# The second half's S5 scan steps, queued behind the last step of the first half's

## The chip, the core and the metric

The kernel runs on one core of one Trainium2 chip, in one launch. The metric is device time in microseconds, the median of several runs. A second number is the profiled execution: one run recorded by the hardware profiler, which gives start, length and releaser of nearly every instruction. The engines named here are TensorE (PE, matrix products into PSUM), VectorE (DVE), ScalarE (ACT), GpSimd (POOL) and SyncE (SP, which issues most loads and stores). Each engine runs its instructions in the order in which they were queued and stops at the first one that has to wait.

## What is computed

One layer of a hybrid backbone over 1024 latent tokens of width 1024, with 256 context tokens ahead of them. Its mixer has two groups, an RG-LRU group and an S5 group; an output projection, a layer norm, a squared-ReLU MLP and a second layer norm follow. The change is in the S5 group. Each of its 64 channel groups of 16 drives a complex diagonal state of 64, forward and backward:

```python
def s5_direction(u_ctx, u_lat, ...):
    lam_bar = jnp.exp(lam * dt)
    def run(u, h0):
        bu = einsum('blgh,gph->blgp', u, b_bar)
        h, h_fin = linear_scan(a, bu, h0, reverse)   # h[t] = a * h[t-1] + bu[t]
        return einsum('blgp,ghp->blgh', h, c_mat).real, h_fin
    y_ctx, h_fin = run(u_ctx, 0)
    y_lat, _ = run(u_lat, h_fin)

s5 = gelu(yl_f + yl_b + d_skip * s_lat)
s5_lat = s5 * sigmoid(s5 @ s5_glu_w + s5_glu_b)      # the GLU
out = concat([rg_lat, s5_lat]) @ w_out + b_out
```

## The kernel before

Products that need more precision than one pass are split: a weight or input x is stored as a high part `h` (a cast by ScalarE, as `wh`) and a low part `l = x - h` (by VectorE, as `wl`), and TensorE adds three products of the parts.

The S5 sequence is cut into chunks of 8 tokens, 32 chunks of context and 128 of latent tokens. TensorE first makes each chunk's contribution to the state (`s5_in`), which lies in two tiles, H0 for the first 32 channel groups and H1 for the other 32. `scan(hf)` then runs over the chunks of one half on VectorE. The 32 context chunks are combined as a tree (tiles `sC`). The latent chunks come one after the other, 127 steps for each half, and each step is three small instructions that need each other's results: `sT` = a * h[i-1], `sU` = the sum of two parts of `sT`, and h[i] = `sU` + h[i].

`s5_states(m)` copies the states of block m out of H0 (m = 0 to 3) or H1 (m = 4 to 7) into a tile `h2`: four copies for each block, all on ScalarE for H0, and half on ScalarE and half on VectorE for H1. `s5_out(m)` multiplies them on TensorE (`ps_so`), applies gelu on ScalarE (`gs`), transposes on TensorE (`ps_gt`), and splits the result into high (ScalarE) and low (VectorE) parts in G0 or G1. G0 takes the memory of H0 and G1 that of H1. The first two output blocks of the GLU are accumulated as the blocks of G come (`ps_gl`); these stand in TensorE's queue between the S5 outputs.

While the scans run, TensorE has other work: the gate projections (`proj_gate`, whose results `ge` VectorE multiplies and SyncE stores), and then the RG-LRU half of the output projection. Its inputs `mh0` to `mh7` are split like weights. Its output blocks are made as the first two together (`k_outer`), four one by one (`prod`), and blocks 6 and 7 together again. Each result in PSUM (`ps_wo`, two buffers for each tag) is evicted by ScalarE to a tile `pt` (`put_part`).

The order on each engine is not the order of the code. A scheduler places every instruction by its own estimate of the times; program order decides between instructions only in part. `with after(x)` tells it that what is issued inside must be queued behind the instruction x. It does not reorder anything while the kernel runs.

Of the kernel before, what the change touches and what calls it, by code (L numbers as in the profile page):

```python
# [15 lines left out]
P = 128  # L16
# [10 lines left out]
GH = 32  # L27
# [14 lines left out]
def build(nc, tc, a, out):  # L42
    V, S, G, PE = nc.vector, nc.scalar, nc.gpsimd, nc.tensor
    MUL, ADD, SUB, MAX = ALU.mult, ALU.add, ALU.subtract, ALU.max

    def tt(o, x, y, op, eng=None):
        (eng or V).tensor_tensor(out=o, in0=x, in1=y, op=op)  # L47
# [13 lines left out]
    def after(ins):  # L61
        return nullcontext() if ins is None else tc.issue_after(ins.ins)
# [120 lines left out]
    def tmp(w=64, dt=F32):  # L183
        cnt[0] += 1
        return pp.tile([P, row(w)], dt, name=f"t{cnt[0]}")[:, 0:w]

    def exp_(v, w):
        k, r, h, e = tmp(w), tmp(w), tmp(w), tmp(w)
        ts(k, v, 1.0 / math.log(2.0), MUL, -127.0, MAX)
        ts(k, k, 127.0, ALU.min, 12582912.0, ADD)  # L190
        ts(k, k, 12582912.0, SUB)
        stt(r, k, -0.693145751953125, v, MUL, ADD)
        stt(r, k, -1.42860682030941723212e-6, r, MUL, ADD)
        ts(r, r, 0.5, ALU.min, -0.5, MAX)
        ts(h, r, 1.0 / 40320, MUL)
        for n in (5040, 720, 120, 24, 6, 2, 1):
            stt(h, h, 1.0 / n, r, ADD, MUL)
        ts(h, h, 1.0, ADD)
        ts(k, k, 127.0, ADD, 8388608.0, MUL)
        ei = tmp(w, I32)  # L200
        V.tensor_copy(ei, k)
        tt(e, h, f(ei), MUL)
        return e
# [77 lines left out]
    u, z, z2, acc = tmp(16), tmp(16), tmp(16), tmp(16)  # L281
    S.activation(u, lam, AF.Abs)
    ts(u, u, -1.0, MUL)
    u = exp_(u, 16)
# [22 lines left out]
    for k in range(KT):  # L307
# [18 lines left out]
        for r, src, pl_, n in ((0, xr, xlp, NL), (1, xc, xcp, NC)):  # L326
            h = pl_.tile([P, n], F32R, name=f"x{r}h{k}")
            lo = pl_.tile([P, n], F32R, name=f"x{r}l{k}")
            t = sup.tile([P, n], F32, tag=f"xt{r}", name="xt", bufs=1)
# [262 lines left out]
    def s5_in(m):  # L592
        ub = inp.tile([P, 8, NCH], F32, tag="ub", name="ub", bufs=2)
        ld(ub, uscr[m].rearrange("t (c g) n -> (t c) g n", g=8))
        for q in range(2):
            xt = inp.tile([P, 4, 2, P], F32, tag="xt", name="xt", bufs=3)
            in_ld[m] = ld(xt, xscr[m, q])
            for g in range(4):
# [6 lines left out]
                cp(hv[64:128, :, 0:CC], ps[64:128, :, CC - 1::-1])  # L605
                cp(hv[64:128, :, CC:NCH], ps[64:128, :, NCH - 1:CC - 1:-1])

    def scan(hf):
        h = H[hf]
        hs = slice(hf * GH, (hf + 1) * GH)  # L610

        for q in range(5):
            d = 1 << q
            for o in range(0, CC, 16 * d):
                n = min(8, (CC - o) // (2 * d))
                lo, hi = (h[:, o + e:o + e + 2 * d * (n - 1) + 1:2 * d] for e in (d - 1, 2 * d - 1))
                t = [pst.tile([P, 8, 2, GH], F32, tag="tr", name="sC", bufs=2)[:, 0:n] for _ in range(2)]
                tt(t[0], a8[:, q, 0:1, hs].unsqueeze(1).to_broadcast([P, n, 2, GH]), lo, MUL)
                tt(t[1], a8[:, q, 1:3, hs].unsqueeze(1).to_broadcast([P, n, 2, GH]), lo, MUL)
                tt(hi, t[0], hi, ADD)  # L620
                tt(hi, t[1][:, :, ::-1, :], hi, ADD)
        al = sc.tile([P, 2, 2, GH], F32, tag=f"al{hf}", name=f"al{hf}", bufs=1)
        V.tensor_copy(al[:, 0], a8[:, 0, 0:1, hs].to_broadcast([P, 2, GH]))
        V.tensor_copy(al[:, 1], a8[:, 0, 1:3, hs])
        for i in range(CC, NCH - 1):
            t = sc.tile([P, 2, 2, GH], F32, tag=f"sT{hf}", name="sT", bufs=2)
            tt(t, al, h[:, i - 1:i].to_broadcast([P, 2, 2, GH]), MUL)
            u = sc.tile([P, 2, GH], F32, tag=f"sU{hf}", name="sU", bufs=2)
            tt(u, t[:, 0], t[:, 1, ::-1, :], ADD)
            tt(h[:, i], u, h[:, i], ADD)  # L630


    def proj_gate(m):
# [95 lines left out]
    def s5_states(m):  # L729
        h2 = h2s[m] = sop[m % 4 // 3].tile([P, 8, 2, CL], F32, tag="h2", name="h2", bufs=3 if m % 4 < 3 else 1)  # L730
        for q in range(2):
            starts(H[m // 4], h2[:, 4 * q:4 * q + 4], (m % 4) * 8 + 4 * q, V.tensor_copy if m >= 4 else S.copy)

    def s5_out(m):
        if m % 2 == 0:
            mtt[m // 2] = sop[1].tile([P, 16, P], F32, tag="mt", name="mt", bufs=2)
            kv = kpscr[m // 2].rearrange("m (g c) x -> c (m g) x", g=8)
            for t in range(T8):
                ld(mtt[m // 2][16 * t:16 * t + 16], kv[:, :, (8 - t) * 16:(8 - t) * 16 + P])
        mt = mtt[m // 2][:, 8 * (m % 2):8 * (m % 2) + 8]  # L740
        u2 = sop[1].tile([P, 8, CL], F32, tag="u2", name="u2", bufs=3)
        ld(u2, uscr[m].rearrange("t (c g) n -> (t c) g n", g=8)[:, :, CC:NCH])
        yf = sop[1].tile([P, 2, 2, 4, P], F32, tag="yf", name="yf", bufs=3)
        ld(yf, yscr[m])
        h2 = h2s[m]
        gs = sc.tile([P, T8, 8, 16], F32, tag="gs", name="gs", bufs=2)
        for s in range(2):
            ps = psx.tile([P, 4, P], F32, tag="si", name="ps_so", bufs=2)
            for g in range(4):
                gl = 4 * s + g  # L750
                PE.matmul(ps[:, g, :], u2[:, gl, :], mt[:, gl, :], start=True, stop=False)
                PE.matmul(ps[:, g, :], h2[:, gl, 0, :], yf[:, s, 0, g, :], start=False, stop=False)
                PE.matmul(ps[:, g, :], h2[:, gl, 1, :], yf[:, s, 1, g, :], start=False, stop=True)
            S.activation(gs[:, :, 4 * s:4 * s + 4].rearrange("n t g c -> n g t c"),
                         ps.rearrange("n g (t c) -> n g t c", t=T8), AF.Gelu_apprx_tanh)
        hl = glin[m]
        for j in range(2):
            pt = pst.tile([P, 4, P], F32, tag="tr", name="ps_gt", bufs=2)
            for t in range(4):
                PE.transpose(pt[:, t, :], gs[:, 4 * j + t].rearrange("n g c -> n (g c)"), ident)  # L760
            pf = pt.rearrange("p t n -> p (t n)")
            S.copy(hl[:, 0, HS[j]], pf)
            tt(hl[:, 1, HS[j]], pf, f(hl[:, 0, HS[j]]), SUB)

    for hf in range(2):
        if hf == 0:
            scan(0)
        for m in range(4 * hf, 4 * hf + 4):
            s5_states(m)
        if hf == 0:  # L770
            scan(1)

        g = hp_[hf].tile([P, 5, 2, NL], F32R, tag="h", name=f"G{hf}", bufs=1)
        for m in range(4):
            glin[4 * hf + m] = g[:, m]
        for m in range(4):
            s5_out(4 * hf + m)
# [294 lines left out]
    for p in range(0, NP1 + 4, 2):  # L1072
# [7 lines left out]
        for e in range(2):  # L1080
# [3 lines left out]
            t = ap_.tile([P, 512], F32, tag="r", name="p2", bufs=3)  # L1084
# [75 lines left out]
    def rt():  # L1160
        return ap_.tile([P, 512], F32, tag="r", name="r", bufs=3)
# [5 lines left out]
    for n, p in stream:  # L1167
# [4 lines left out]
        if n == "1":  # L1172

            h = a2.tile([P, 4, 512], F32, tag="hq", name="hq", bufs=2)
            u = a1.tile([P, 2, 512], F32, tag="u", name="u", bufs=2)
            v, t = p2t.pop(p), rt()
# [272 lines left out]
def program(arrays):  # L1449
    import concourse.bacc as bacc  # L1450

    nc = bacc.Bacc("TRN2", target_bir_lowering=False, num_devices=1, dynamic_dma_scratch_size=1024)
    aps = {n: nc.dram_tensor(f"in_{n}", v.shape, mybir.dt.from_np(v.dtype), kind="ExternalInput").ap() for n, v in arrays.items()}
    out = nc.dram_tensor("out_0", (D, NL), F32, kind="ExternalOutput").ap()
    with tile.TileContext(nc) as tc:
        build(nc, tc, aps, out)
    return nc
# [10 lines left out]
```

## Time and profile before

| | us |
|---|---|
| median of 3 runs | 1590.09 (1587.28 to 1592.53) |
| profiled execution | 1590.72 |
| its span, first to last instruction | 1588.9 |
| TensorE busy | 1481.7 (93%) |
| VectorE busy | 1241.8 (78%) |
| ScalarE busy | 859.1 (54%) |

The time outside the span is 1.8 us. A busy share is an average over stages, so it says which engine to follow and not where time is lost. For that one reads the stretches and the waits of single instructions. In a row of the timeline the number in brackets at the end is the idle time of the engine ahead of that instruction and what ended it. Rows that begin before the row above has ended are normal, since the instructions of an engine are pipelined; the distance from start to start is the time that an instruction takes from the queue.

### The profile page before, as it was taken

To read this page: it belongs to the slowest core of one execution; us is meant where nothing else is said; L and a number is where in the kernel's file an instruction comes from. 1 tells how busy PE (TensorE), PEld (TensorE's weight loads), DVE (VectorE), ACT (ScalarE), POOL (GpSimd) and SP (SyncE) were. 2 spreads that over 40 slices of the span, in tenths; PEclk is the share of its full clock that TensorE was granted. 3 is DMA by queue.
4 is the path that set the end of the run, shared out by engine and by line. 5 is a ranking of instruction groups with operands and counts; after the bars stand their busy time and mean duration, and the time that the engine had idled before them with its cause. 6 is when DMAs were issued, how large, how long until landed. Compare 5 with 4: busy or idle time off the path is not lost. (4 is left out here: it accounts for less than half of the span.)

```text
span 1588.9 us, 20498 instructions
## 1 busy us (share of the span) xinstructions
PE 1481.7 (93%) x7148; PEld 1207.3 (76%) x7148; DVE 1241.8 (78%) x2523; ACT 859.1 (54%) x1210; POOL 54.1 (3%) x101
## 2 busy tenths in 40 slices
PE   7899998999978999699999898999999999999997
PEld 2687777778866878598878666877887788888787
DVE  7899899999876989644978788777876556757867
ACT  4676656676795331964233467555656544344325
POOL 0000000000000000000000011010111000000000
PEclk9999999999999999899999899999999999999998
DMA  7623333323664762983768576999997876776603
GB/s 257 230 95 118 104 112 110 106 104 133 218 222 141 199 192 96 251 186 122 241 209 276 153 237 218 311 294 295 290 303 199 312 266 214 260 253 198 230 7 106
DMA packets 143831, 312.56 MB, mean 197 GB/s; under 512 B 16496, under 2 KB 47728, under 8 KB 142320
## 3 DMA queue, kind: packets, MB, share of 16 engines
q1 hardware_dynamic: 104048, 237.45, 46.4%
q10 hardware_dynamic: 31360, 52.83, 8.9%
q0 software_dynamic: 8320, 20.98, 6.0%
q8 instruction: 56, 0.92, 0.2%
q14 instruction: 47, 0.39, 0.1%
HBM read 227.91 MB, written 83.30 MB: 196 GB/s over the span
## 5 line engine op out<-in xcount | busy, mean ns | idle before, releaser
L98 ACT CAST wh<-wr 128x1024 fp32r<-128x1024 f32 x113 | 118.4, 1051 | 235.6 <-PE ps_m L1280 78.4
L47 DVE TENSOR_TENSOR wl<-wr,wh 128x1024 fp32r<-128x1024 f32 (+1 forms) x129 | 148.7, 1154 | 76.3 <-ACT wh L98 76.0
L1280 PE MATMUL ps_m<-bh,wh 128*128 128x512 f32 x392 | 155.1, 396 | 5.8 <-ACT bh L1242 3.7
L1066 PE MATMUL ps_m<-xt,wh 128*128 128x512 f32 x512 | 157.7, 390 | 0.0
L1280 PE MATMUL ps_m<-bl,wh 128*128 128x512 f32 x392 | 154.3, 394 | 0.0
L1280 PE MATMUL ps_m<-bh,wl 128*128 128x512 f32 x392 | 154.0, 393 | 0.0
L380 PE MATMUL ps_mm<-x0h,wh 128*128 128x512 f32 x352 | 141.5, 402 | 1.0 <-ACT wh L98 1.0
L380 PE MATMUL ps_mm<-x0h,wl 128*128 128x512 f32 x352 | 141.5, 403 | 0.9 <-DVE wl L47 0.9
L380 PE MATMUL ps_mm<-x0l,wh 128*128 128x512 f32 x352 | 140.7, 400 | 0.0
L1066 PEld LDWEIGHTS ps_m<-xt,wh 128*128 128x128 f32 x512 | 96.1, 188 | 20.4
L1066 PE MATMUL ps_m<-xt,wl 128*128 128x512 f32 x256 | 99.6, 390 | 0.2 <-DMA wl<-in_w 0.2
L1280 PEld LDWEIGHTS ps_m<-bh,wh 128*128 128x128 f32 x392 | 74.5, 190 | 23.9 <-ACT bh L1242 4.1
L1280 PEld LDWEIGHTS ps_m<-bl,wh 128*128 128x128 f32 x392 | 74.6, 190 | 16.4 <-DVE bl L47 0.8
L1280 PEld LDWEIGHTS ps_m<-bh,wl 128*128 128x128 f32 x392 | 74.6, 190 | 15.6
L675 PE MATMUL ps_wo<-ms,wh 128*128 128x512 f32 x256 | 82.0, 401 | 1.8 <-DVE ms L47 1.0
L1066 PE MATMUL ps_m<-x,wh 128*128 128x512 f32 x256 | 82.2, 402 | 0.0
L380 PEld LDWEIGHTS ps_mm<-x0h,wl 128*128 128x128 f32 x352 | 67.8, 193 | 14.5 <-DVE wl L47 1.4
L380 PEld LDWEIGHTS ps_mm<-x0h,wh 128*128 128x128 f32 x352 | 67.8, 193 | 13.7 <-ACT wh L98 1.4
L380 PEld LDWEIGHTS ps_mm<-x0l,wh 128*128 128x128 f32 x352 | 67.8, 193 | 12.8
L47 DVE TENSOR_TENSOR u<-ps_m,u 128x512 f32<-128x512 f32 (+1 forms) x60 | 49.6, 831 | 34.3 <-PE ps_m L1066 33.9
L47 DVE TENSOR_TENSOR sT<-al,H 128x128 f32<-128x128 f32 x254 | 66.1, 281 | 1.3
L47 DVE TENSOR_TENSOR bl<-br,bh 128x1024 fp32r<-128x1024 f32 x49 | 59.5, 1218 | 2.0 <-ACT bh L1242 2.0
(348 smaller groups left out, 3707.6 us busy)
## 6 DMA issues: line engine op xcount, KB each, us to landing
wr<-in_w SPq DMA_DIRECT2D x79, 512.0 KB, 5.3
br<-hq SPq DMA_DIRECT2D x49, 512.0 KB, 4.9
mo<-in_ada_t SPq DMA_DIRECT2D x32, 512.0 KB, 3.8
hq<-hs ACTq DMA_DIRECT2D x14, 1024.0 KB, 10.1
wr<-in_w_in SPq DMA_DIRECT2D x24, 512.0 KB, 4.1
wr<-in_w_out SPq DMA_DIRECT2D x24, 512.0 KB, 4.6
xt<-xt ACTq DMA_DIRECT2D x16, 512.0 KB, 2.7
yd<-Y SPq DMA_DIRECT2D x16, 512.0 KB, 2.6
```

The source lines that it names most:

```text
L47: (eng or V).tensor_tensor(out=o, in0=x, in1=y, op=op)
L98: S.copy(hi, raw)
L380: PE.matmul(ps, w[:, ks], x, start=(k == 0 and c == 0), stop=(k == KT - 1 and c == 2))
L675: PE.matmul(ps, u[:, ks], v[:, js], start=(c == 0), stop=(c == 3 * KT - 1))
L1066: PE.matmul(ps, u[:, ks], v, start=(first and c == 0), stop=(last and c == 11))
L1280: PE.matmul(pss[m], w[:, 512 * k + P * m:512 * k + P * m + P], x[:, 512 * k:512 * k + 512], start=(q == 0 and k == 0 and c == 0), stop=(q ...
```

## The change

The steps of a scan are issued behind the last step of the scan before it, and `scan(1)` stands in the code directly behind `scan(0)`, ahead of the state copies of blocks 0 to 3. The tree over the context chunks has no such order. No instruction is added or taken away, and nothing is computed in another way. The lines of `scan` lie two to four further down in the changed file, and those behind it four.

```diff
@@ -605,6 +605,8 @@
                 cp(hv[64:128, :, 0:CC], ps[64:128, :, CC - 1::-1])
                 cp(hv[64:128, :, CC:NCH], ps[64:128, :, NCH - 1:CC - 1:-1])
 
+    scan_end = [None]
+
     def scan(hf):
         h = H[hf]
         hs = slice(hf * GH, (hf + 1) * GH)
@@ -624,10 +626,12 @@
         V.tensor_copy(al[:, 1], a8[:, 0, 1:3, hs])
         for i in range(CC, NCH - 1):
             t = sc.tile([P, 2, 2, GH], F32, tag=f"sT{hf}", name="sT", bufs=2)
-            tt(t, al, h[:, i - 1:i].to_broadcast([P, 2, 2, GH]), MUL)
+            with after(scan_end[0]):
+                V.tensor_tensor(out=t, in0=al, in1=h[:, i - 1:i].to_broadcast([P, 2, 2, GH]), op=MUL)
             u = sc.tile([P, 2, GH], F32, tag=f"sU{hf}", name="sU", bufs=2)
             tt(u, t[:, 0], t[:, 1, ::-1, :], ADD)
-            tt(h[:, i], u, h[:, i], ADD)
+            end = V.tensor_tensor(out=h[:, i], in0=u, in1=h[:, i], op=ADD)
+        scan_end[0] = end
 
 
     def proj_gate(m):
@@ -765,10 +769,9 @@
     for hf in range(2):
         if hf == 0:
             scan(0)
+            scan(1)
         for m in range(4 * hf, 4 * hf + 4):
             s5_states(m)
-        if hf == 0:
-            scan(1)
 
         g = hp_[hf].tile([P, 5, 2, NL], F32R, tag="h", name=f"G{hf}", bufs=1)
         for m in range(4):
```

The orders of TensorE, GpSimd and SyncE are unchanged. VectorE's and ScalarE's are changed from the first latent step of H1 to the last state copies.

VectorE, at the first latent step of H1, before (`al0` and `al1` are the coefficients of the halves; every number is that of a buffer):

```order
L47 TENSOR_TENSOR sT_5457<-al0_5344,H0_3774 128x128
L47 TENSOR_TENSOR sT_6041<-al1_6038,H1_3775 128x128
L47 TENSOR_TENSOR sU_5459<-sT_5457 128x64
L47 TENSOR_TENSOR sU_6043<-sT_6041 128x64
L47 TENSOR_TENSOR H0_3774<-sU_5459,H0_3774 128x64
L47 TENSOR_TENSOR H1_3775<-sU_6043,H1_3775 128x64
L47 TENSOR_TENSOR sT_5462<-al0_5344,H0_3774 128x128
L47 TENSOR_TENSOR sT_6046<-al1_6038,H1_3775 128x128
L47 TENSOR_TENSOR sU_5464<-sT_5462 128x64
```

and now:

```order
L630 TENSOR_TENSOR sT_5457<-al0_5344,H0_3774 128x128
L47 TENSOR_TENSOR sU_5459<-sT_5457 128x64
L633 TENSOR_TENSOR H0_3774<-sU_5459,H0_3774 128x64
L630 TENSOR_TENSOR sT_5462<-al0_5344,H0_3774 128x128
L47 TENSOR_TENSOR sU_5464<-sT_5462 128x64
L633 TENSOR_TENSOR H0_3774<-sU_5464,H0_3774 128x64
L630 TENSOR_TENSOR sT_5467<-al0_5344,H0_3774 128x128
L47 TENSOR_TENSOR sU_5469<-sT_5467 128x64
L633 TENSOR_TENSOR H0_3774<-sU_5469,H0_3774 128x64
```

The steps of the two halves took turns; now H0's stand alone, and those of H1 follow behind the 127th of H0. The weight splits and gate products still stand between them.

ScalarE, around the evictions of output blocks 4 (`pt_5103`) and 5 (`pt_5164`), before:

```order
L681 COPY pt_5103<-ps_wo_5053 128x512
L98 CAST wh_5177<-wr_5175 128x1024
L681 COPY pt_5103<-ps_wo_5078 128x512
L683 DMA pt4_5106<-pt_5103 128x1024
L681 COPY pt_5164<-ps_wo_5114 128x512
L98 CAST wh_5298<-wr_5296 128x1024
L681 COPY pt_5164<-ps_wo_5139 128x512
L724 COPY h2_5982<-H0_3774 64x1024
L683 DMA pt5_5167<-pt_5164 128x1024
```

and now (`h2_6656` is block 0's states, `h2_6661` block 1's):

```order
L685 COPY pt_5103<-ps_wo_5053 128x512
L728 COPY h2_6656<-H0_3774 64x1024
L729 COPY h2_6656<-H0_3774 64x1024
L728 COPY h2_6656<-H0_3774 64x1024
L729 COPY h2_6656<-H0_3774 64x1024
L728 COPY h2_6661<-H0_3774 64x1024
L98 CAST wh_5177<-wr_5175 128x1024
L685 COPY pt_5103<-ps_wo_5078 128x512
L729 COPY h2_6661<-H0_3774 64x1024
```

The first state copies stand ahead of the second eviction of block 4 where they stood behind both evictions of block 5. The copies of block 2 now stand between the two evictions of block 5.

VectorE, at the end of H1's scan, before (`wl_5305` and `wl_7229` are GLU weights, `ps_gt_6719` and `ps_gt_6726` the transposed output of block 0):

```order
L47 TENSOR_TENSOR sU_6673<-sT_6671 128x64
L47 TENSOR_TENSOR H1_3775<-sU_6673,H1_3775 128x64
L47 TENSOR_TENSOR wl_5305<-wr_5302,wh_5304 128x1024
L47 TENSOR_TENSOR wl_7229<-wr_7226,wh_7228 128x1024
L725 COPY h2_6883<-H1_3775 64x1024 x2
L47 TENSOR_TENSOR G0_6676<-ps_gt_6719,G0_6676 128x512
L47 TENSOR_TENSOR G0_6676<-ps_gt_6726,G0_6676 128x512
```

and now, where the same low parts of G0 stand:

```order
L47 TENSOR_TENSOR sU_6498<-sT_6496 128x64
L633 TENSOR_TENSOR H1_3775<-sU_6498,H1_3775 128x64
L630 TENSOR_TENSOR sT_6501<-al1_6018,H1_3775 128x128
L47 TENSOR_TENSOR G0_6676<-ps_gt_6719,G0_6676 128x512
L47 TENSOR_TENSOR sU_6503<-sT_6501 128x64
L47 TENSOR_TENSOR G0_6676<-ps_gt_6726,G0_6676 128x512
L633 TENSOR_TENSOR H1_3775<-sU_6503,H1_3775 128x64
L630 TENSOR_TENSOR sT_6506<-al1_6018,H1_3775 128x128
```

The low parts of block 0 followed the last step of H1; now they stand among H1's steps, behind the 96th. Those of block 1 stand seven steps later, and those of blocks 2 and 3 behind the last.

## Rows read from the trace of the kernel before

**Rows 1.** The page: span, and TensorE's busy time, share and instructions
```profile
span 1588.9 us, 20498 instructions
...
PE 1481.7 (93%) x7148; PEld 1207.3 (76%) x7148; DVE 1241.8 (78%) x2523; ACT 859.1 (54%) x1210; POOL 54.1 (3%) x101
```

**Rows 2.** Stretches: us; busy us (instructions) of PE, PEld, DVE, ACT, POOL; clock, DMA, GB/s
```profile
600.00:630.00 30.00, 30.00 (x132) 24.48 (x131) 30.00 (x173) 4.83 (x7) 0.00 (x0) 1.00 0.28 94
662.40:675.40 13.00, 0.00 (x0) 0.00 (x0) 1.73 (x2) 12.89 (x13) 1.11 (x2) 0.63 1.13 322
675.40:679.40 4.00, 3.99 (x18) 3.99 (x19) 3.64 (x4) 3.05 (x4) 0.00 (x0) 0.50 0.27 115
683.60:740.00 56.40, 56.40 (x424) 52.10 (x422) 16.93 (x20) 25.39 (x32) 0.00 (x0) 1.00 0.71 179
```

**Rows 3.** VectorE in time order (start us, us, line, tiles): steps of H1 alone
```profile
640.66 0.23 DVE L47 TENSOR_TENSOR H<-sU,H 128x64 f32<-128x64 f32 x1
...
660.96 0.23 DVE L47 TENSOR_TENSOR H<-sU,H 128x64 f32<-128x64 f32 x1
```

**Rows 4.** VectorE: steps of both halves in turn
```profile
513.71 0.48 DVE L47 TENSOR_TENSOR sT<-al,H 128x128 f32<-128x128 f32 x2
...
517.50 0.49 DVE L47 TENSOR_TENSOR sT<-al,H 128x128 f32<-128x128 f32 x2
```

**Rows 5.** VectorE: a weight split, a gate product, the low parts of mix 5 and 7
```profile
518.65 1.21 DVE L47 TENSOR_TENSOR wl<-wr,wh 128x1024 fp32r<-128x1024 f32 x1
519.78 0.68 DVE L47 TENSOR_TENSOR ge<-ge 128x512 f32<-128x512 f32 x1
...
570.33 1.22 DVE L47 TENSOR_TENSOR mh<-mraw,mh 128x1024 fp32r<-128x1024 f32 x1
...
578.35 1.22 DVE L47 TENSOR_TENSOR mh<-mraw,mh 128x1024 fp32r<-128x1024 f32 x1 [2.71 <-ACT mh L662]
```

**Rows 6.** ScalarE in time order: evictions, state copies, casts and gelu
```profile
614.58 0.59 ACT L681 COPY pt<-ps_wo 128x512 f32<-128x512 f32 x1 [4.22 <-PE ps_wo L675]
...
638.66 2.08 ACT L724 COPY h<-H 64x1024 f32<-64x1024 f32 x1 [6.22 <-DVE H L47]
...
663.09 0.59 ACT L681 COPY pt<-ps_wo 128x512 f32<-128x512 f32 x1
...
666.08 1.92 ACT L724 COPY h<-H 64x1024 f32<-64x1024 f32 x1
...
673.81 1.04 ACT L98 CAST wh<-wr 128x1024 fp32r<-128x1024 f32 x1
674.76 1.08 ACT L754 ACTIVATE gs<-ps_so 128x512 f32<-128x512 f32 x2
```

**Rows 7.** TensorE in time order: where each stage begins
```profile
586.78 0.63 PE L675 MATMUL ps_wo<-mh,wh 128*128 128x512 f32 x2
...
625.42 0.63 PE L675 MATMUL ps_wo<-mh,wh 128*128 128x512 f32 x2
...
630.94 0.62 PE L694 MATMUL ps_wo<-mh,wh 128*128 128x512 f32 x2
...
652.71 0.40 PE L694 MATMUL ps_wo<-mh,wl 128*128 128x512 f32 x1
...
675.41 0.80 PE L751 MATMUL ps_so<-mt,u 128*128 128x128 f32 x2 [13.01 <-ACT gs L754]
...
683.63 0.71 PE L694 MATMUL ps_gl<-G,wh 128*128 128x512 f32 x2
...
690.33 0.61 PE L751 MATMUL ps_so<-mt,u 128*128 128x128 f32 x4
...
695.69 0.39 PE L751 MATMUL ps_so<-mt,u 128*128 128x128 f32 x2
...
708.58 0.61 PE L751 MATMUL ps_so<-mt,u 128*128 128x128 f32 x4
```

## Prediction

> **What bounds the kernel now.** The page first: TensorE is busy 1481.7 of a span of 1588.9 us [rows 1], so time is lost only where TensorE is kept waiting. Then the stretches around the change: from 600 to 630 us TensorE and VectorE are both busy without a gap, and from 662.4 to 675.4 TensorE does nothing while ScalarE is busy 12.89 of 13.00 us [rows 2]. The waits on TensorE's row say the same: 13.01 us before the S5 output of block 1, released by ScalarE's gelu `gs` [rows 7]. ScalarE is late there because twelve state copies `h2` from H0 started at 638.66, after a wait of 6.22 us for VectorE's last scan step of H0, and four more came before the gelu [rows 6]. So two things count: when VectorE ends each scan, and what stands behind the copies on ScalarE.
>
> **One step alone, one step of a pair.** A scan step is three dependent VectorE instructions (sT, sU, H). Alone, 24 of them took from 640.66 to 660.96: 0.846 us each [rows 3]. Interleaved, a pair (one step of H0, one of H1) took (517.50 - 513.71) / 4 = 0.948 us [rows 4]. The partner costs 0.10, since each instruction fills the time in which the other chain waits for its own result. The change takes the partners apart: all 127 steps of H1 stand behind the 127th of H0. Some 103 steps of H1 ran beside one of H0 before, and each will cost 0.846 and not 0.10.
>
> The Trainium skill, "VectorE: DVE Perf Modes", section "The DRAIN you can't avoid" with its rules for authors, says that chained instructions pay a drain each whatever the waits, so only their number matters. By that a lone step would cost half a pair. That is rival B below. The rows here disagree: 0.846 against 0.474.
>
> **VectorE up to the end of H0.** The order is the same up to 513.71. From there to the low part of mix 5 there stand 58 lone steps of H0 (49.1 us), where 48 of H0 and 46 of H1 stood in pairs, with nine `ge` products of at most 0.68 and four `wl` splits of 1.13 as before [rows 5]: 513.71 + 49.1 + 6.1 + 4.5 = 573.4, 3.1 later than 570.33. The low part of mix 7 waited for ScalarE's cast; its load uses the buffer that mix 5 gives back (there are three), so I shift it by all of the 3.1, from 579.6 to 582.7 (bound: not at all). TensorE wants it in the last eighth of a projection that ends at 586.78 [rows 7], so in its last 2.8 us, from 584.0: this costs nothing. Then 45 lone steps (38.1) and five `wl` (5.7): H0 is ready at 626.5, where the trace has 638.66: 12 us earlier.
>
> **ScalarE and TensorE behind it.** Now the copies stand further forward: five of them between the first and the second `pt` eviction of output block 4. ScalarE is free at 615.2 and waits for H0. Five copies at 2.04 (twelve took 638.66 to 663.09), a cast of 0.95 and an eviction of 0.6 [rows 6]: the second `pt` is done at 626.5 + 10.2 + 1.5 = 638.2. TensorE's next product takes the PSUM buffer that this eviction frees. It started at 625.42 [rows 7] and will start at 638.2, 12.8 late. It takes 5.5, and 2.0 for the clock: after the 13 us pause the granted clock was 0.50 (1.2 GHz) for 4.0 us [rows 2]. So it ends at 645.7.
> Meanwhile ScalarE does three copies, one eviction, four copies, a cast, an eviction: 638.2 + 6.1 + 0.6 + 8.2 + 0.95 + 0.6 = 654.6. TensorE needs that last eviction after nine matmuls of blocks 6 and 7 (645.7 + 2.1 = 647.8), and waits 6.8. The whole of them, 96, took 630.94 to 652.95 [rows 7], 0.229 each: the other 87 give 19.9, clock 2.0, end at 676.5, 23.5 late.
> Then come two evictions (two more and a cast lie beside TensorE's last matmuls), four copies (1.93 each), a cast, the gelu: 676.5 + 1.2 + 7.7 + 0.95 + 0.6 = 687.0. The S5 output of block 0 (652.95 to some 662.4 before) lies beside this. So block 1 starts at 687.0, in place of 675.41: 11.6 late. Of the old wait of 13.01 little is left, but 19.6 of new waits stand ahead of it.
>
> **VectorE through H1.** `wl` splits stand between the steps, and wait for casts that now stand behind copies on ScalarE. From 626.5: 8 steps to 633.3; `wl` waits for the cast at 637.7 and ends at 638.8; 13 steps to 649.8; `wl` waits for 654.0, ends 655.1; 26 steps to 677.1; `wl` to 678.2; 6 steps to 683.3; `wl` waits for the cast at 686.4, ends 687.5; 43 steps to 723.9. Only there do the low parts of G0's block 0 stand (two, which I take at 0.68 as the `ge` of the same size): 725.3. Seven steps to 731.2, block 1's low parts to 732.6, 24 steps to **752.9**: H1 is ready 91.7 us later than in the trace, 661.19 [rows 3]. The waits in this are 4.4 + 4.2 + 3.1 = 11.7; bounds are none of it and twice it.
>
> **TensorE through the S5 outputs.** GLU block 0 is reached 11.6 after 683.63, at 695.2, and waits for the low part at 724.6: 29 us. Two GLU blocks take 6.7 (683.63 to 690.33) [rows 7]; the second, of 2.8 without the transposes, waits for 731.9 and ends at 734.7. S5 output 2 takes 5.4: 740.1. Output 3 needs the PSUM buffer that the gelu of output 2 frees, and that gelu stands on ScalarE behind four copies of H1, which now wait for 752.9: 752.9 + 8.2 + 0.6 = 761.7. The trace has 695.69: 66.0 late. From there the trace needs 12.9 to the start of S5 output 4 (708.58). Add 2.0 for the clock after the 22 us pause, and at a guess half a copy, 1.0, because GLU block 3's high parts come behind a copy on ScalarE: 777.6, **69.0 us late**. Behind it both orders are the same on every engine, and TensorE had no gap from 683.6 to 740 [rows 2]: nothing there can be given back.
>
> **Sum.** The profiled execution took 1590.72 (its span and 1.8 around it), so 1659.7. The median of the timed runs is 1590.09, 0.6 less: I forecast **1659 us**.
>
> **Rivals.**
> A. VectorE's waits in H1 do not come, because casts are earlier than I place them. H1 ends at 741.2 and everything behind it follows: 11.7 less, 1647. For it: I place casts by ScalarE's queue, which rests on H0's end and on TensorE's new waits. Against: those `wl` stand at fixed places among H1's steps, and the casts at fixed places behind copies.
> B. A lone step costs half a pair, 0.474. H0 would be ready at 579.6 + 21.3 + 5.7 = 606.6, before ScalarE asks (615.2), so ScalarE's queue decides: the same sum from 615.2 starts block 1 at 675.5, where it was. VectorE's last `wl` would end at 676.0; 74 steps (35.1) and four low parts (2.7) later H1 is ready, 713.8. Copies and gelu to 722.6 against 695.69, and 3.0 as above: 29.9 late, 1620. Against it: 24 rows at 0.846.
> C. Not slower: H0's earlier end takes away the 13.01 wait, and H1's end is hidden behind TensorE's GLU and S5 work. Price -13.0, 1578. It decides from the point that H1 ends before GLU block 1 does (690.33), beside which ScalarE first asks for it; from 626.5, with four `wl` and no wait, that leaves (63.8 - 4.5) / 127 = 0.467 a step. The rows give 0.846.
> D. More is lost: TensorE's pauses each cost more clock than 2.0, the GLU weights' loads slip, VectorE waits twice as much. 11.7 more, 1671. It begins where those pauses sum to over 5 us more. For it: four long pauses where there was one. Against: loads of weights are issued long before.
>
> **How the numbers follow.** Forecast 0.70 (1652 to 1665), A 0.14, D 0.10, B 0.03, C 0.02, and 0.01 for no change at all. I let the range reach to both neighbours, 1642 to 1672, which leaves out about one in ten. 0.3% is 4.8 us, about what a measurement of this kernel can tell from no change. Faster has C's 0.02, same 0.01, slower the rest, 0.97.
>
> **What would show it.** Right: scan steps of H0 and H1 at 0.85 each, H0 ready near 626, H1 near 753; on TensorE a wait of some 12 us for `pt` near 626, one of 7 near 648, one of 29 for the low part of G0 near 695, one of 21 for `gs` near 740; S5 output 4 near 778, and from there the same time to the end as before. Wrong: lone steps well under 0.8 (then B or C), no wait at the `wl` splits in H1 (A), or a TensorE row after 780 that has new gaps (D). The forecast would be wrong altogether if ScalarE ran its copies past the evictions, as its queue does not allow.

## The result, and the profile after

The changed kernel takes 1653.34 us (median of four runs, 1652.48 to 1656.99), the kernel before 1590.87 in the same rounds: 1.041 times as long, 95% interval 1.0384 to 1.0437. The forecast was 1659 us, slower. When S5 output 4 begins, at 773.39 in place of 708.58 [rows 7], it is 64.8 us late; 3.0 of that comes back later, which leaves the 61.8 by which the span grew.

The page of the kernel after, span and first row (busy us, share, instructions):

```profile
span 1650.7 us, 20497 instructions
...
PE 1481.9 (90%) x7148; PEld 1205.3 (73%) x7148; DVE 1294.1 (78%) x2523; ACT 857.9 (52%) x1210; POOL 54.0 (3%) x101
```

TensorE is busy as long as before [rows 1], so what is new is waiting. VectorE runs the same 2523 instructions and is busy 52 us longer, which fits steps that overlapped a partner and now stand alone.

VectorE after, in time order (start us, us, line, tiles): the low part of mix 7; the last step of H0 and two of H1, a step of which begins in the row `sT`; then two `wl` splits in H1's scan, two step ends that lie 24 steps apart, the first low part of G0, the last step, and the copies behind it (the rows write the tile `h2` as `h`):

```profile
579.27 1.23 DVE L47 TENSOR_TENSOR mh<-mraw,mh 128x1024 fp32r<-128x1024 f32 x1 [1.02 <-ACT mh L666]
...
624.14 0.22 DVE L633 TENSOR_TENSOR H<-sU,H 128x64 f32<-128x64 f32 x1
...
624.86 0.22 DVE L633 TENSOR_TENSOR H<-sU,H 128x64 f32<-128x64 f32 x1
625.12 0.29 DVE L630 TENSOR_TENSOR sT<-al,H 128x128 f32<-128x128 f32 x1
625.44 0.22 DVE L47 TENSOR_TENSOR sU<-sT 128x64 f32<-128x64 f32 x1
625.70 0.22 DVE L633 TENSOR_TENSOR H<-sU,H 128x64 f32<-128x64 f32 x1
...
635.07 1.23 DVE L47 TENSOR_TENSOR wl<-wr,wh 128x1024 fp32r<-128x1024 f32 x1 [3.75 <-ACT wh L98]
...
651.30 1.22 DVE L47 TENSOR_TENSOR wl<-wr,wh 128x1024 fp32r<-128x1024 f32 x1 [4.12 <-ACT wh L98]
...
653.54 0.22 DVE L633 TENSOR_TENSOR H<-sU,H 128x64 f32<-128x64 f32 x1
...
673.84 0.23 DVE L633 TENSOR_TENSOR H<-sU,H 128x64 f32<-128x64 f32 x1
...
721.73 0.68 DVE L47 TENSOR_TENSOR G<-ps_gt,G 128x512 fp32r<-128x512 f32 x1
...
749.34 0.23 DVE L633 TENSOR_TENSOR H<-sU,H 128x64 f32<-128x64 f32 x1
749.60 7.41 DVE L729 COPY h<-H 64x1024 f32<-64x1024 f32 x6
```

A step of H1 alone takes 625.70 - 624.86 = 0.84 us, and 24 of them from 653.54 to 673.84 take 0.846 each, as the lone ones did before [rows 3]. H0 ends at 624.4 (before 638.66), H1 at 749.6 (before 661.19). Each instruction is busy 0.22 to 0.29, and the next starts 0.26 to 0.32 after it.

ScalarE after, in time order: copies, casts and evictions behind H0, and the copies of H1 ahead of a gelu `gs`:

```profile
612.74 0.58 ACT L685 COPY pt<-ps_wo 128x512 f32<-128x512 f32 x1 [4.21 <-PE ps_wo L679]
624.39 1.94 ACT L728 COPY h<-H 64x1024 f32<-64x1024 f32 x1 [11.06 <-DVE H L633]
...
634.00 1.04 ACT L98 CAST wh<-wr 128x1024 fp32r<-128x1024 f32 x1
634.94 0.57 ACT L685 COPY pt<-ps_wo 128x512 f32<-128x512 f32 x1
...
651.17 0.58 ACT L685 COPY pt<-ps_wo 128x512 f32<-128x512 f32 x1
...
749.60 7.38 ACT L728 COPY h<-H 64x1024 f32<-64x1024 f32 x4 [23.15 <-DVE H L633]
756.88 1.06 ACT L758 ACTIVATE gs<-ps_so 128x512 f32<-128x512 f32 x2
```

TensorE after, in time order: its rows with a wait of over 1 us, with the wait and who ended it in brackets, and the start of S5 output 4:

```profile
635.57 1.22 PE L679 MATMUL ps_wo<-mh,wh 128*128 128x512 f32 x2 [11.82 <-ACT pt L685]
651.80 1.22 PE L698 MATMUL ps_wo<-mh,wh 128*128 128x512 f32 x2 [6.08 <-ACT pt L685]
685.18 0.79 PE L755 MATMUL ps_so<-mt,u 128*128 128x128 f32 x2 [4.95 <-ACT gs L758]
722.47 0.80 PE L698 MATMUL ps_gl<-G,wh 128*128 128x512 f32 x1 [28.98 <-DVE G L47]
729.34 0.50 PE L698 MATMUL ps_gl<-G,wh 128*128 128x512 f32 x1 [1.26 <-DVE G L47]
757.52 0.80 PE L755 MATMUL ps_so<-mt,u 128*128 128x128 f32 x2 [19.97 <-ACT gs L758]
...
773.39 0.61 PE L755 MATMUL ps_so<-mt,u 128*128 128x128 f32 x4
```

Three stretches after, each from the end of a wait of TensorE (columns as in [rows 2]; the granted clock is the third number from the end):

```profile
635.57:643.52 7.95, 7.95 (x25) 6.43 (x25) 7.06 (x28) 7.88 (x5) 0.00 (x0) 0.68 0.40 135
651.80:674.70 22.90, 22.90 (x87) 18.46 (x88) 19.99 (x79) 1.90 (x3) 0.00 (x0) 0.87 0.76 176
757.52:773.39 15.87, 15.87 (x88) 14.45 (x89) 5.34 (x6) 11.28 (x11) 0.00 (x0) 0.81 0.42 58
```

The stretch before that answers to the last of them, from S5 output 3 to S5 output 4:

```profile
695.69:708.58 12.89, 12.89 (x91) 11.46 (x90) 7.90 (x8) 11.22 (x11) 0.00 (x0) 1.00 0.89 199
```

The one wait of 13.01 [rows 7] has become six, 73.1 us together. The reader should not add them up as six prices: the experiments show that one time, H1's end, sets most of the sum, and that the waits are only where TensorE meets it.

### The profile page after: what moved, and what is told of

Same layout as the page of the kernel before. It is cut to its first block, busy times and chain, and to the rows that moved or that the text cites. A ratio compares the mean times of both kernels' runs of the same rounds, so it can differ in the third digit from the quotient of the medians.

```text
span 1650.7 us, 20497 instructions
## 1 busy us (share of the span) xinstructions
PE 1481.9 (90%) x7148; PEld 1205.3 (73%) x7148; DVE 1294.1 (78%) x2523; ACT 857.9 (52%) x1210; POOL 54.0 (3%) x101
## 5 line engine op out<-in xcount | busy, mean ns | idle before, releaser
L630 DVE TENSOR_TENSOR sT<-al,H 128x128 f32<-128x128 f32 x254 | 74.1, 292 | 8.1
L380 PEld LDWEIGHTS ps_mm<-x0h,wl 128*128 128x128 f32 x352 | 67.3, 191 | 14.3 <-DVE wl L47 1.4
L633 DVE TENSOR_TENSOR H<-sU,H 128x64 f32<-128x64 f32 x254 | 57.2, 225 | 8.3
```

Source lines behind the costliest of these rows:

```text
L380: PE.matmul(ps, w[:, ks], x, start=(k == 0 and c == 0), stop=(k == KT - 1 and c == 2))
L630: V.tensor_tensor(out=t, in0=al, in1=h[:, i - 1:i].to_broadcast([P, 2, 2, GH]), op=MUL)
L633: end = V.tensor_tensor(out=h[:, i], in0=u, in1=h[:, i], op=ADD)
```

## Experiments

Theory: steps without a partner cost 0.846 us, H1 ends about 90 us later, and that end decides. Rivals: the new place of `scan(1)` in the code; the waits as costs of their own, from ScalarE's and VectorE's order; a step price that goes by the number of instructions.

### e1: the place in the code alone

```diff
         if hf == 0:
             scan(0)
+            scan(1)
...
-        if hf == 0:
-            scan(1)
```

> One part of the change alone: scan(1) stands in the code directly behind scan(0), without the queueing of its steps behind H0's. Theory (the loss is the loss of the partner steps, so it comes from the queueing alone): H0's and H1's steps still take turns, and the time is that of the kernel before, 1591 us, within 3 us. Rival (it is the place in the code that moves the state copies and H1's end): some or all of the 62 us, 1610 to 1653.

Measured: 1587.84 us against 1587.58, ratio 1.0004 (0.9988 to 1.002). The place in the code alone does nothing, and the order of every engine was that of the kernel before. So the loss needs the queueing of the steps; queueing with `scan(1)` left in its old place was not run.

### e2: the low parts of G0 earlier, H1's copies later

```diff
+            if hf and i == CC + 62:
+                scan_end[0] = end
+                yield
...
+            low = V.tensor_tensor(out=hl[:, 1, HS[j]], in0=pf, in1=f(hl[:, 0, HS[j]]), op=SUB)
+        if m == 0:
+            scan_end[0] = low
...
+            rest = scan(1)
+            next(rest)
...
+            if m == 0 and hf == 0:
+                list(rest)
```

> The changed kernel, but H1's steps from the 63rd on are issued behind the S5 output of block 0 and queued behind its low parts, so that the low parts of block 0 stand behind 62 steps of H1 and not 96, those of blocks 2 and 3 also ahead of H1's end, and H1's copies on ScalarE stand behind all four gelus of the first half. The waits of 29 us (low part of G0) and of 20 us (gelu behind H1's copies) go from their places. Theory (H1's end decides, the waits are only where TensorE meets it): H1 ends later by the four more low parts ahead of it, 749.6 + 2.9 = 752.5; eight copies on ScalarE at 1.85 and the gelu of S5 output 4 then free its buffer at 768, where S5 output 5 began at 779.5 in the changed kernel: 11.5 gained of 49, 1641 us; TensorE waits instead at S5 outputs 4 and 5. Rival (the waits are each a cost of their own and add up): 1652.5 - 29 - 20 = 1604.

Measured: 1643.04 us, ratio to before 1.0352 (1.033 to 1.0375). TensorE in e2:

```profile
705.79 0.50 PE L701 MATMUL ps_gl<-G,wh 128*128 128x512 f32 x1 [3.06 <-DVE G L770]
737.48 0.80 PE L701 MATMUL ps_gl<-G,wh 128*128 128x512 f32 x1 [16.91 <-DVE G L770]
...
758.98 0.80 PE L759 MATMUL ps_so<-yf,h 128*128 128x128 f32 x2 [11.32 <-ACT h L731]
772.35 0.80 PE L758 MATMUL ps_so<-mt,u 128*128 128x128 f32 x2 [6.66 <-ACT gs L761]
```

The wait of 29 us is 3.1 here and that of 20 is gone, but 16.9 stand at block 2's low part and 18.0 at S5 outputs 4 and 5. Of 49 us 10.3 were gained by the medians and 9 by the ratios, where the theory expected 11.5. The waits do not add up.

### e3: ScalarE's evictions first

```diff
+    last_pt = [None]
...
-            S.copy(t[:, HS[j]], ps)
+            last_pt[0] = S.copy(t[:, HS[j]], ps)
...
-            starts(H[m // 4], h2[:, 4 * q:4 * q + 4], ...)
+            with after(last_pt[0] if m < 4 else None):
+                starts(H[m // 4], h2[:, 4 * q:4 * q + 4], ...)
```

> The changed kernel, but the sixteen state copies from H0 are queued behind the last eviction pt of output block 7, so ScalarE does all evictions of the RG-LRU half first. Theory: TensorE's waits of 11.8 and 6.1 us for pt are gone and blocks 6 and 7 end near 652, but the sixteen copies (1.93 each, 31 us) then stand from there ahead of the first gelu, so S5 output 1 starts at 687 as it did (685). What is gained is only VectorE's waits at the wl splits in H1 (3.75, 4.1 and most of 3.5), so H1 ends at about 740 in place of 749.6 and the time is 1643 us, 10 less. Rival (TensorE's early waits are a cost of their own): 18 less, 1635, or with both 1625.

Measured: 1639.06 us, ratio to before 1.0329 (1.0303 to 1.0355). VectorE in e3, the first two `wl` splits in H1's scan:

```profile
631.09 1.22 DVE L47 TENSOR_TENSOR wl<-wr,wh 128x1024 fp32r<-128x1024 f32 x1
643.08 1.22 DVE L47 TENSOR_TENSOR wl<-wr,wh 128x1024 fp32r<-128x1024 f32 x1
```

TensorE in e3, at S5 output 1 and GLU block 0:

```profile
686.63 0.80 PE L758 MATMUL ps_so<-mt,u 128*128 128x128 f32 x2 [18.73 <-ACT gs L761]
711.27 0.80 PE L700 MATMUL ps_gl<-G,wh 128*128 128x512 f32 x1 [15.25 <-DVE G L47]
```

ScalarE in e3, the first copies of H1:

```profile
738.42 7.38 ACT L730 COPY h<-H 64x1024 f32<-64x1024 f32 x4 [23.16 <-DVE H L633]
```

Both early waits of TensorE, 17.9 us, are gone, and S5 output 1 starts no sooner (686.63 against 685.18): its own wait is 18.73 where it was 4.95. The four `wl` splits wait 0.6 us in all, in place of 11.7, and H1 ends at 738.4, 11.2 earlier. The time fell by 14.3 by the medians and 13 by the ratios, between the theory's 10 and the rival's 18, so the time alone does not decide. The rows do: nothing was gained up to S5 output 1, 11.2 at H1's end, and 12.2 when S5 output 4 begins (761.16 against 773.39).

### e4: half of H1's steps

```diff
-        for i in range(CC, NCH - 1):
+        for i in range(CC, NCH - 1 - 64 * hf):
```

> The changed kernel with 64 of H1's 127 latent steps left out (the states of the last 64 latent chunks stay without what comes from the chunks ahead of them). Theory (each lone step costs 0.846 us, and H1's end decides): H1 ends 54 us earlier, at 695; the low parts of G0's block 0 come at about 698 and GLU block 0 waits 5 us for them in place of 29; from there as in the kernel before, 25 us to S5 output 4, at 724 in place of 773. 49 us less, 1604. Rival (a lone step costs half a pair, 0.474, and something else is late): 64 steps give back 30 us, 1622. Rival (the end is set by ScalarE's copies and evictions, whatever H1 does): less than 10 us given back.

Measured: 1604.26 us, ratio to before 1.0113 (1.0082 to 1.0143). 49 us went with 64 steps by the medians and 47 by the ratios, 0.77 or 0.74 us each on the whole time. ScalarE shows H1's end at its first copy:

```profile
696.69 1.93 ACT L728 COPY h<-H 64x1024 f32<-64x1024 f32 x1 [8.06 <-DVE H L633]
```

With H0's first copy at 628.57 in this run, H1 takes 68.1 us behind H0; it took 749.60 - 624.39 = 125.2. The difference is 57.1. 64 steps at 0.845 (54.1), the four low parts, which now stand behind the scan (2.9), and 1.0 less of waits at the `wl` splits make 58.0, so the price of a lone step is met within 2%. This is the plainest evidence that the lone steps set the time. TensorE no longer waited for the low parts here: at GLU block 0 it waited 1.93 us (to 699.16) for a cast by ScalarE, where the theory had 5 for a low part.

### e5: two chains of half the width

```diff
+            cs = (slice(0, GH // 2), slice(GH // 2, GH))
+            for c in cs:
+                with after(scan_end[0]):
+                    V.tensor_tensor(out=t[:, :, :, c], in0=al[:, :, :, c], ...)
+            for c in cs:
+                tt(u[:, :, c], t[:, 0, :, c], t[:, 1, ::-1, c], ADD)
+            for c in cs:
+                end = V.tensor_tensor(out=h[:, i, :, c], in0=u[:, :, c], ...)
```

> The changed kernel with each half's latent scan cut into two independent chains of 16 channel groups, whose instructions take turns: six instructions of half the width to a step in place of three. Theory (a lone step is long because each instruction waits for the result of the one ahead of it): a partner chain fills the wait, so six instructions cost what a lone step or a pair of full width cost, 0.85 to 0.95 us, and the time stays between 1645 and 1680 us. Rival (each instruction has a fixed cost, with or without a partner, so only their number matters): six cost twice a lone step, 1.69; some 230 lone steps of both halves then cost 195 us more, far over 1800 us.

Measured: 1631.8 us, ratio to before 1.0299 (1.0255 to 1.0344), 18 us less than the changed kernel by the ratios and 21.5 by the medians. VectorE in e5 (each row two instructions, one of each chain):

```profile
717.14 0.31 DVE L637 TENSOR_TENSOR H<-sU,H 128x32 f32<-128x32 f32 x2
717.37 0.35 DVE L633 TENSOR_TENSOR sT<-al,H 128x64 f32<-128x64 f32 x2
717.64 0.31 DVE L47 TENSOR_TENSOR sU<-sT 128x32 f32<-128x32 f32 x2
717.86 0.31 DVE L637 TENSOR_TENSOR H<-sU,H 128x32 f32<-128x32 f32 x2
```

TensorE in e5, at GLU block 0:

```profile
719.32 0.79 PE L702 MATMUL ps_gl<-G,wh 128*128 128x512 f32 x1 [30.09 <-DVE G L47]
```

A step of six instructions takes 717.86 - 717.14 = 0.72 us, less than the three of full width alone (0.845). So it is not the number of instructions that makes a lone step long, but the wait of each for the result ahead of it; an independent partner fills it. H1 ended 106.8 us behind H0 (ScalarE's first copies at 612.62 and 719.40), where it took 125.2. The rival's 1.69 is refuted, and my 0.85 to 0.95, and with it the 1645 to 1680 us, was too high: at half the width an instruction behind a partner costs 0.12, where it costs 0.158 at full width. The whole time is no second measure of the step: in this order the low parts of G0's block 0 stand behind nearly all of H1's steps, and TensorE still waited 30.09 us for them.

### e6 and e7: the kernel before, with fewer state copies on ScalarE

The wait of 13.01 us before the change is ScalarE's doing, and rival C was right on that. Two ways to relieve it, with the steps in turn as before (the first added line is e6's, the second e7's):

```diff
-            starts(..., V.tensor_copy if m >= 4 else S.copy)
+            starts(..., V.tensor_copy if m >= 2 else S.copy)
+            starts(..., V.tensor_copy if m >= 4 else G.tensor_copy)
```

> The kernel before (steps of both halves in turn), with the second copies of blocks 2 and 3 of H0, four in all, on VectorE in place of ScalarE. Theory: TensorE's wait of 13.0 us for the gelu at S5 output 1 is set by ScalarE's sixteen copies; two of the four copies after the evictions and two before go, 7.9 us less on ScalarE. VectorE pays 4 x 1.3 us, two of them ahead of H1's last 20 steps, so H1 ends 2.7 later, at 664, before it is asked for. 1582 to 1586 us. Rival (TensorE's next bound, the low parts of G0 on VectorE behind H1's end, takes its place): no gain, 1588 to 1591.

Measured for e6: 1579.93 us against 1587.44, ratio 0.996 (0.9943 to 0.9978), the one version that beats both kernels. ScalarE in e6, the first gelu:

```profile
668.51 1.09 ACT L754 ACTIVATE gs<-ps_so 128x512 f32<-128x512 f32 x2 [2.21 <-DMA pt<-pt]
```

TensorE in e6, at S5 output 1:

```profile
669.17 0.79 PE L751 MATMUL ps_so<-mt,u 128*128 128x128 f32 x2 [8.59 <-ACT gs L754]
```

S5 output 1 starts at 669.17, 6.2 earlier than at 675.41 [rows 7]. No wait at G0's low parts takes its place, so that rival falls. The time lies below the 1582 to 1586 expected, which counted a gain of 4 to 8 from 1590; the gain was 7.5 by the medians and 6.4 by the ratios. S5 output 4 began 5.5 earlier (703.11 against 708.58 [rows 7]); what more there is lies behind it, where the orders are the same. The next limit is the DMA that empties the tile `pt`, whose buffer the gelu takes: it ended the gelu's last 2.21 us of waiting.

> The kernel before, with the second copy of each pair of state copies of H0 (eight of 64x1024) on GpSimd, which has nothing else to do there, in place of ScalarE. Theory: ScalarE has eight copies (16 us) less ahead of the gelu of S5 output 0, so TensorE's wait of 13.0 us at S5 output 1 goes, and 10 to 13 us are gained: 1576 to 1580 us, if a copy on GpSimd takes under 4 us, which no row shows. Rival (copies on GpSimd are slower than that, or slow VectorE's steps beside them): S5 output 0 or 1 waits for GpSimd, no gain or a loss, 1588 to 1605.

Measured for e7: 1586.9 us, ratio 1.0001 (0.9982 to 1.002): no gain, the rival. VectorE in e7, before and beside the copies on GpSimd:

```profile
639.87 0.23 DVE L47 TENSOR_TENSOR sU<-sT 128x64 f32<-128x64 f32 x1
...
641.61 2.03 DVE L47 TENSOR_TENSOR H<-sU,H 128x64 f32<-128x64 f32 x1
643.68 2.00 DVE L47 TENSOR_TENSOR sT<-al,H 128x128 f32<-128x128 f32 x1
645.71 1.93 DVE L47 TENSOR_TENSOR sU<-sT 128x64 f32<-128x64 f32 x1
```

GpSimd in e7, the first six copies:

```profile
640.50 13.04 POOL L725 COPY h<-H 64x1024 f32<-64x1024 f32 x6 [73.40 <-DVE H L47]
```

TensorE in e7, at GLU block 0:

```profile
679.69 0.79 PE L694 MATMUL ps_gl<-G,wh 128*128 128x512 f32 x1 [8.18 <-ACT G L762]
```

Each VectorE instruction of the scan beside these copies took some 2.0 us, about as long as a copy (13.04 / 6 = 2.17). H1 ended at 677.1 in place of 661.2, ScalarE's copies of H1 waited for it, and TensorE waited at GLU block 0 for a cast behind them, in place of S5 output 1.

## Why the prediction was right

- **Price of a lone step.** Forecast 0.846, measured 0.84 to 0.846 in the kernel after, and 57.1 us for 64 of them with the four low parts in e4. The Trainium skill, "VectorE: DVE Perf Modes", section "The DRAIN you can't avoid" with its rules for authors, has chained instructions pay a drain each whatever the waits. That does not hold for this chain: three instructions alone took 0.845 and six in two chains 0.72. The same section of the Trainium skill also says that a next instruction which is not held starts earlier; the 0.12 from start to start in e5's two chains agrees with that.
- **H0 ready.** Forecast 626.5, measured 624.4. The miss is in one term: I shifted the low part of mix 7 by 3.1, to 582.7, and it ended at 580.50, 0.9 later than before. From there to H0's end it took 43.9, forecast 43.8. In e2 and e4, whose orders up to there are those of the kernel after, ScalarE's first copy came at 629.63 and 628.57, so that a hit within 2.1 us is in part luck.
- **ScalarE's and TensorE's middle.** Forecast waits of 12.8 and 6.8 for `pt`, measured 11.82 and 6.08: a copy took 1.94 where I took 2.04. S5 output 1 forecast at 687.0, measured at 685.18. The place of each wait was right; as prices of their own they were worth nothing up to S5 output 1 (e3).
- **VectorE's waits in H1.** Forecast 4.4, 4.2 and 3.1, together 11.7; measured 3.75, 4.12, 0.30 and 3.54, together 11.7. That the sums agree to the tenth is luck, since three waits became four. Rival A had none. e3 took them away, and H1 ended 11.2 earlier.
- **H1's end and what hangs on it.** Forecast 752.9, measured 749.6: 2.1 of that is H0's. The low part of G0 forecast for 724.6, TensorE went on at 722.47 after 28.98 (forecast 29). S5 output 3 forecast 761.7, measured 757.52: 3.3 from H1's end, 0.8 from H1's four copies, 7.38 where I took 8.2. From there to S5 output 4 it took 15.87 us, forecast 15.9, but its two extra terms were wrong by 1.0 each and cancel, which is luck: TensorE was busy for all of the 15.87 us, at a granted clock of 0.50 (1.2 GHz) for the first 6 us and 1.00 behind them, 0.81 in the mean; 15.87 x 0.81 is 12.9, the time of the kernel before at 1.00. So the clock cost 3.0 where I took 2.0, and the guessed half copy cost nothing.
- **What comes behind.** I took it as unchanged. From S5 output 4 to the end of the span it is 1650.7 - 773.39 = 877.3, before 880.3. The order there is the same, and e1, whose orders are all those of the kernel before, took 1586.9 - 708.94 = 878.0. So the 3.0 is a difference between runs and not an effect of the change (1577.25 to 1594.59 for the kernel before, over all rounds).

So the profiled execution was forecast 7.2 us too high (1659.7 against 1652.5): 4.2 of sizes up to S5 output 4 and 3.0 behind it. The median was forecast 5.7 too high, since it lies 0.9 above the profiled execution where I took it 0.6 below. Rival C (not slower) needed 0.467 a step; it was right only in that the old wait was worth taking away, which e6 does. D was right that pauses cost more clock than 2.0: by the stretches above 7.95 x 0.32 = 2.5 after the first, 22.90 x 0.13 = 3.0 after the second, and the 3.0 ahead of S5 output 4. Behind the first two, shorter copies and H0's earlier end made up for it (S5 output 1 began 1.8 ahead of its forecast), and the third was offset by the half copy, so that D's further loss did not come.

## What to carry to other kernels

A chain of small dependent instructions on one engine can be priced by the wait of each for the one ahead, and an independent chain queued between its instructions can be nearly free, as here (0.10 of 0.846 us); before two such chains are put one behind the other, find out who waits for the end of the second. When one late result shows up as several waits on the busiest engine, moving or removing a wait may only move it to the next place that needs the result. An idle engine is no free helper until its effect on the neighbours is seen.

## What the runs showed of the hardware

- Half the width and twice the instructions made a VectorE chain faster, 0.72 against 0.845 us a step, when the halves took turns (e5).
- While GpSimd's copies of 64x1024 ran, VectorE's small instructions with two inputs went from 0.22 to 0.29 us to some 2.0 (e7). The Trainium skill, "Advanced Engine Details and Errata", section "GPSIMD Details", says that GpSimd shares a read and a write interface with VectorE and conflicts with its instructions that have two inputs in SBUF. The rows agree with that, and give the size of it: beside six copies, 13.04 us, VectorE finished six scan instructions.
